# Convolution statistics from partial sums, issued one step later, and q projections pulled up beside the last LayerNorm

## The chip, the cores and the metric

The kernel runs on all eight cores of one Trainium2 chip, one batch element per core, with no exchange between cores. The metric is the device time of one launch, set by the slowest core. Such a program has a second, slower state in some executions: the cores of one die show a lower granted TensorE clock (0.834 to 0.838 in one run of the changed kernel). Ratios compare fast runs alone. A median given here is of all runs of its kernel, slow ones included, unless it is called one of fast runs. The kernel before takes 1239.6 us (median of 16 runs, 1235.1 the fastest; three of the 16 lie above 1300 us, and the median of the other 13 is 1238.8).

## The reference, cut to what matters

One encoder layer for `x` of 2048 x 1024 per core:

```python
x = layer_norm(x, ln_in_g, ln_in_b)
u = x @ w_in                                   # q | k | v | conv-GLU | gates
y_a = windowed_gqa(q, k, v, rel_bias, sink) @ w_attn_out
# conformer branch: GLU, depthwise conv of width 31, LayerNorm over 512 channels, SiLU
y_c = silu(layer_norm(depthwise(glu) + conv_b, conv_ln_g, conv_ln_b)) @ w_conv_out
mix = (sigmoid(g_a) * y_a + sigmoid(g_c) * y_c) @ w_out
# ... two more LayerNorms and a SwiGLU feed-forward ...
```

The change touches the LayerNorm of the conformer branch and the order of what follows it up to attention.

## The kernel before

A small scheduler keeps one list of operations per engine and derives semaphores from what each operation reads and writes. Every engine works through its own list in order. An operation that waits holds up everything behind it on its engine. Names: `pe` is TensorE, `act` ScalarE, `dve` VectorE, `pool` GpSimd. `tc` counts four blocks of 512 tokens, `cc` four tiles of 128 channels. A PSUM bank is one 128 x 512 fp32 piece of the memory into which TensorE writes its products; to evict it is to copy it out, after which TensorE may use it again.

```python
for tc in range(4):                            # one convolution block
    for cc in range(4):
        pb = 4 + (cc % 2)                      # two PSUM banks
        # pe: 31 matmuls with diagonal weights into bank(pb)
        # act: dv[cc] = bank(pb) + bias ; act: sqv[cc] = dv[cc]**2        [cut]
    def f_mean(e, dv=dv):                      # mean over partitions and tiles: 4 fp32 products
        for cc in range(4):
            ins = e.matmul(bank(6), onesm[:, :], dv[:, cc, :], start=(cc == 0), stop=(cc == 3))
        return ins
    sc.add("pe", f_mean, ...)                  # f_ex2: the same 4 products on sqv into bank 7
    # act: m2b = mean**2 ; dve: varb = ex2 - m2b ; act: rstdb = sqrt ; dve: reciprocal
    # per cc: dve subtract, dve multiply, act SiLU -> ycin                [cut]
# pool: memset of esf (overlays the buffers above); dve: sink terms       [cut]
for j in range(3):                             # bias tables, one staging pair
    sc.dma("sp", ... out=bstage ...)           # and mstage
    sc.add("act", ... exp(bstage) ...)
    sc.add("dve", ... expb[j] = bstage * mstage ...)
wslots = [load_w(c) for c in range(4)]         # q weights, issued by pool
for i in range(4):                             # 16 q tiles
    for tc in range(4):
        pb = nextbank(0, 4)
        proj(wslots[i], 0, 128, tc, pb, 128)   # pe: 8 matmuls
        # act: copy bank(pb) to qT                                        [cut]
# then 4 k tiles, 4 v tiles, attention; then the gates (wao, wco loads)   [cut]
```

The softmax here doesn't subtract the row's maximum and nothing guards it: scores larger than these inputs give would overflow.

Of the kernel before, what the change touches and what calls it, by code (L numbers as in the profile page):

```python
# [5 lines left out]
F32 = mybir.dt.float32  # L6
BF16 = mybir.dt.bfloat16
# [3 lines left out]
S = 2048  # L11
# [173 lines left out]
def build(debug=False):  # L185
# [80 lines left out]
    def bank(b):  # L266
        return ps[:, b * 512:(b + 1) * 512]
# [249 lines left out]
    tbuf, o = sbn(o, 2, [128, 512], F32, "tbuf")  # L517
    for tc in range(4):
# [4 lines left out]
        for cc in range(4):  # L523
            pb = 4 + (cc % 2)

            def f_conv(e, cc=cc, tc=tc, pb=pb):
                ins = None
                for j in range(31):
# [9 lines left out]
                   reads=[(dn, cc)], writes=[("sq", cc)])  # L538

        def f_mean(e, dv=dv):  # L540
            ins = None
            for cc in range(4):
                ins = e.matmul(bank(6), onesm[:, :], dv[:, cc, :], start=(cc == 0), stop=(cc == 3))
            return ins
        sc.add("pe", f_mean, reads=[(dn, c) for c in range(4)] + ["onesm"], writes=[("ps", 6)])

        def f_ex2(e, sqv=sqv):
            ins = None
            for cc in range(4):
                ins = e.matmul(bank(7), onesm[:, :], sqv[:, cc, :], start=(cc == 0), stop=(cc == 3))  # L550
            return ins
        sc.add("pe", f_ex2, reads=[("sq", c) for c in range(4)] + ["onesm"], writes=[("ps", 7)])
        sc.add("act", lambda e: e.activation(m2b[:, :], bank(6), AF.Square), reads=[("ps", 6)], writes=["m2b"])
        sc.add("dve", lambda e: e.tensor_tensor(varb[:, :], bank(7), m2b[:, :], ALU.subtract),  # L554
               reads=[("ps", 7), "m2b"], writes=["varb"])
        sc.add("act", lambda e: e.activation(rstdb[:, :], varb[:, :], AF.Sqrt, bias=epsc[:, 0:1]),
               reads=["varb", "epsc"], writes=["rstdb"])
        sc.add("dve", lambda e: e.reciprocal(rstdb[:, :], rstdb[:, :]), reads=["rstdb"], writes=["rstdb"])
        for cc in range(4):
            tb = tbuf[cc % 2]  # L560
            tn = "tbuf%d" % (cc % 2)
            sc.add("dve", lambda e, cc=cc, tb=tb, dv=dv: e.tensor_tensor(tb[:, :], dv[:, cc, :], bank(6), ALU.subtract),
                   reads=[(dn, cc), ("ps", 6)], writes=[tn])
            sc.add("dve", lambda e, tb=tb: e.tensor_tensor(tb[:, :], tb[:, :], rstdb[:, :], ALU.mult),
                   reads=[tn, "rstdb"], writes=[tn])
            sc.add("act", lambda e, cc=cc, tc=tc, tb=tb: e.activation(
                ycv[:, cc, tc * 512:(tc + 1) * 512], tb[:, :], AF.Silu,
                bias=small[:, C_CONVLB + cc:C_CONVLB + cc + 1], scale=small[:, C_CONVG + cc:C_CONVG + cc + 1]),
                reads=[tn, "small"], writes=[("ycin", cc)])
    dbg_dump("d_ycin", ycin, 128, 4 * S)  # L570

    o = MT_OFF
    qT, o = sb(o, [128, 8 * S], BF16, "qT")
    assert o <= AD_OFF
# [9 lines left out]
    NP = 9  # L584
    pTb, o = sbn(o, NP, [128, 512], BF16, "pT")
# [3 lines left out]
    qTv = qT[:, :].rearrange("p (h s) -> p h s", h=8)  # L589
# [9 lines left out]
    sc.add("act", lambda e: e.activation(esink[0:64, :], small[0:64, C_SINK:C_SINK + 8], AF.Exp),  # L599
           reads=["small"], writes=["esink"])  # L600
    sc.add("pool", lambda e: e.memset(esf[0:64, :], 0.0), writes=["esf"])
    for h in range(8):
        sc.add("dve", lambda e, h=h: e.tensor_scalar(esfv[0:64, h, :], esfv[0:64, h, :], esink[0:64, h:h + 1],
                                                      None, ALU.add), reads=["esf", "esink"], writes=["esf"])
    sc.add("dve", lambda e: e.tensor_copy(esh[0:1, :], esf[0:1, :]), reads=["esf"], writes=["esh"])
    sc.add("dve", lambda e: e.tensor_tensor(esf[0:1, :], esf[0:1, :], esh[0:1, :], ALU.subtract),
           reads=["esf", "esh"], writes=["esf"])
    sc.add("dve", lambda e: e.tensor_copy(esl[0:1, :], esf[0:1, :]), reads=["esf"], writes=["esl"])
    for j in range(3):
        sc.dma("sp", lambda e, j=j: e.dma_start(out=bstage[:, :], in_=bias_d[j]), writes=["bstage"])  # L610
        sc.dma("sp", lambda e, j=j: e.dma_start(out=mstage[:, :], in_=mask_d[j]), writes=["mstage"])
        sc.add("act", lambda e: e.activation(bstage[:, :], bstage[:, :], AF.Exp), reads=["bstage"], writes=["bstage"])
        sc.add("dve", lambda e, j=j: e.tensor_tensor(expbv[:, j, :], bstage[:, :], mstage[:, :], ALU.mult),
               reads=["bstage", "mstage"], writes=["expb"])

    pctr = [0]

    def nextbank(lo, n):
        b = lo + pctr[0] % n
        pctr[0] += 1  # L620
        return b

    wslots = [load_w(c) for c in range(4)]
    sk_ = None
    for i in range(4):
        s_ = wslots[i]
        if i == 1:
            sk_ = load_w(4)
        if i == 2:
            sv_ = load_w(5)  # L630
# [510 lines left out]
```

## Time and profile before

| what | value |
|---|---|
| time, median of 16 runs | 1239.6 us |
| profiled run | 1235.1 us, cores 1219.7 to 1233.6 |
| mean over cores, first convolution matmul to first attention matmul (QK) | 216.8 us |
| mean over cores, first QK to first product with v | 3.38 us |

The profiled run is the fastest of the sixteen. The last row is read from each core's TensorE timeline; I call it "the stretch". The lines that show how it is filled stand in the prediction.

### The profile page before, as it was taken

Reading aid. Unit: us, or ns where it says so; the run is one execution under the profiler, and the core shown is the slowest. Engines: PE = TensorE matmul, PEld = TensorE weight load, DVE = VectorE, ACT = ScalarE, POOL = GpSimd, SP = SyncE. Lnnn points to the kernel's source line nnn. Section 1 sums busy time; section 2 is a strip of 40 time slices with the busy share of each in tenths; the row PEclk is TensorE's granted clock in tenths of the full one; section 3 lists DMA queues with packets and bytes.
Section 4 is the critical chain, followed back from the end, with each engine's and each line's share of the span. In section 5 each row is a group of like instructions: output and inputs, shape, how many; then the busy total and the mean of one; then the engine's idle time right before and its main releaser. Section 6 shows DMA issues by size and latency. Waiting matters only on the chain.

```text
span 1233.6 us, 14722 instructions; the slowest of 8 cores (1219.7 to 1233.6 us)
## 1 busy us (share of the span) xinstructions
PE 1057.2 (86%) x4836; PEld 465.6 (38%) x4836; DVE 509.3 (41%) x702; ACT 411.0 (33%) x575; POOL 209.3 (17%) x318
## 2 busy tenths in 40 slices
PE   0778999965999959999963998998989899999994
PEld 0334444422523324444421443443434344444441
DVE  6663022223079812222273454254534454252224
ACT  2463133323379912222215225122341315221111
POOL 1010000001034412323210322011210212103200
PEclk9989999986979969999985999999999999999997
DMA  9762000005200051313080999357860858429901
GB/s 223 178 139 41 1 1 1 18 0 137 44 1 18 13 108 18 69 35 52 1 205 1 160 152 169 65 109 165 131 109 32 191 88 141 62 66 176 152 1 69
DMA packets 44762, 102.92 MB, mean 83 GB/s; under 512 B 5072, under 2 KB 6736, under 8 KB 44304
## 3 DMA queue, kind: packets, MB, share of 16 engines
q0 software_dynamic: 34848, 68.07, 35.1%
q1 hardware_dynamic: 9840, 33.90, 8.4%
q8 instruction: 41, 0.67, 0.2%
q14 instruction: 33, 0.27, 0.1%
HBM read 159.27 MB, written 8.39 MB: 136 GB/s over the span
## 4 chain that ended last, share of the span: by engine, by line
PE 69%; DMA 11%; DVE 8%; ACT 6%; issue 5%; POOL 0%; SPq 0%; DVEq 0%; ACTq 0%; POOLq 0%
PE ps L973 18%; PE ps L381 15%; PE ps L1007 12%; PE ps L529 5%; PE ps L880 3%; PE ps L784 2%; PE ps L775 2%; DMA xtA<-x 2%; PE ps L700 2%; PE ps L671 2%; DMA xtE<-x 2%; DMA wE<-wg 2%; PE ps L708 2%; DMA wdn<-wd 2%; DVE xtE L933 1%
## 5 line engine op out<-in xcount | busy, mean ns | idle before, releaser
L973 PE MATMUL ps<-mT,wE 128*128 128x512 bf16 x1408 | 312.3, 381 | 8.4 <-DMA wE<-wg 5.9
L381 PE MATMUL ps<-x0T,wbuf 128*128 128x512 bf16 x800 | 197.2, 403 | 39.3 <-DMA wbuf<-win 21.4
L973 PEld LDWEIGHTS ps<-mT,wE 128*128 128x128 bf16 x1408 | 137.2, 98 | 175.7 <-issue 17.0
L1007 PE MATMUL ps<-wdn,hid 128*128 128x512 bf16 x704 | 152.6, 379 | 4.4 <-DVE hid L981 3.0
L381 PEld LDWEIGHTS ps<-x0T,wbuf 128*128 128x128 bf16 x800 | 81.2, 102 | 146.7 <-issue 63.2
L981 DVE TENSOR_TENSOR hid<-ps,sgb 128x512 bf16<-128x512 f32 x88 | 60.4, 690 | 163.9 <-PE ps L973 140.7
L979 ACT ACTIVATE sgb<-ps 128x512 f32<-128x512 f32 x88 | 51.7, 593 | 186.2 <-PE ps L973 186.1
L529 PE MATMUL ps<-glu,diag 128*128 128x512 bf16 x496 | 108.4, 379 | 3.4 <-ACT dwb L534 3.4
L308 POOL DMA_DIRECT2D wE<-wg x88 | 46.6, 529 | 342.5 <-PE ps L973 338.5
L1007 PEld LDWEIGHTS ps<-wdn,hid 128*128 128x128 bf16 x704 | 68.6, 98 | 88.4 <-issue 6.3
L880 PE MATMUL ps<-wout,mT 128*128 128x512 bf16 x256 | 66.2, 419 | 19.3 <-DVE xtE L891 19.3
L686 DVE TENSOR_TENSOR pT<-E,expb 128x512 bf16<-128x512 f32 x61 | 59.8, 1017 | 40.5 <-ACT E L680 37.1
L798 DVE TENSOR_TENSOR t<-ps,gab 128x512 f32<-128x512 f32 x32 | 22.1, 692 | 130.3 <-PE ps L775 130.3
L529 PEld LDWEIGHTS ps<-glu,diag 128*128 128x128 bf16 x496 | 47.9, 97 | 64.3 <-issue 6.5
L308 POOL DMA_DIRECT2D wE<-wu x88 | 46.6, 529 | 106.7 <-PE ps L973 92.4
L802 POOL TENSOR_TENSOR mT<-t,t 128x512 bf16<-128x512 f32 x32 | 40.4, 1262 | 122.3 <-DVE t L800 122.3
L792 ACT ACTIVATE gab<-ps,small 128x512 f32<-128x512 f32 x32 | 22.0, 688 | 101.1 <-PE ps L381 101.1
L1013 DVE SCALAR_TENSOR_TENSOR zb<-xtE,ps 128x512 f32<-128x512 f32 x32 | 22.0, 686 | 80.6 <-PE ps L1007 80.6
L686 POOL TENSOR_TENSOR pT<-E,expb 128x512 bf16<-128x512 f32 x31 | 39.4, 1272 | 77.7 <-ACT E L680 76.0
L880 PEld LDWEIGHTS ps<-wout,mT 128*128 128x128 bf16 x256 | 26.8, 106 | 56.9 <-issue 33.0
L680 ACT ACTIVATE E<-ps 128x512 f32<-128x512 f32 x92 | 47.5, 580 | 0.5 <-POOL pT L686 0.5
L554 DVE TENSOR_TENSOR varb<-ps,m2b 128x512 f32<-128x512 f32 x4 | 2.8, 692 | 104.0 <-PE ps L550 104.0
(112 smaller groups left out, 1069.1 us busy)
## 6 DMA issues: line engine op xcount, KB each, us to landing
wE<-wg POOLq DMA_DIRECT2D x88, 256.0 KB, 5.6
wE<-wu POOLq DMA_DIRECT2D x88, 256.0 KB, 5.7
xtA<-x SPq DMA_DIRECT2D x16, 512.0 KB, 8.9
xtE<-x SPq DMA_DIRECT2D x16, 512.0 KB, 13.3
out<-zb SPq DMA_DIRECT2D x16, 512.0 KB, 2.8
wbuf<-win POOLq DMA_DIRECT2D x26, 256.0 KB, 5.2
wdn<-wd POOLq DMA_DIRECT2D x11, 512.0 KB, 11.5
lnp<-lnp SPq DMA_DIRECT2D x3, 1024.0 KB, 9.5
```

The costliest lines, as they stand in the source:

```text
L308: sc.dma("pool", lambda e: e.dma_start(out=dst_ap, in_=src_ap), reads=reads, writes=writes)
L381: ins = e.matmul(bank(pb)[0:prows, :], w[:, kc, c0:c1], x0Tv[:, kc, tc * 512:(tc + 1) * 512], start=(kc == 0), stop=(kc == 7))
L529: ins = e.matmul(bank(pb), diagv[:, cc, j, :], gluv[:, cc, tc * 512 + j:tc * 512 + j + 512], start=(j == 0), stop=(j == 30))
L671: sc.add("pe", lambda e, g=g, kb=kb, n=n, pb=pb: e.matmul(bank(pb).rearrange("p (a b q) -> p a b q", a=2, b=2), kTv[0:64, g, kb * 128:(kb ...
L680: sc.add("act", lambda e, Et=Et, pb=pb: e.activation(Et[:, :], bank(pb), AF.Exp, scale=0.125), reads=[("ps", pb)], writes=["E%d" % ei])
L686: sc.add(mul_eng, lambda e, Et=Et, pt=pt, j=j, g=g: e.tensor_tensor(pt[:, :], Et[:, :], expbv[:, j, g * 512:(g + 1) * 512], ALU.mult), rea ...
L802: sc.add("pool", lambda e, t1=t1, t2=t2, f=f, tc=tc: e.tensor_tensor(mTv[:, f, tc * 512:(tc + 1) * 512], t1[:, :], t2[:, :], ALU.add), rea ...
L880: ins = e.matmul(bank(pb), mTv[:, kc, t * 128:(t + 1) * 128], woutv[:, kc, half * 512:(half + 1) * 512], start=(kc == 0), stop=(kc == 7))
L973: ins = e.matmul(bank(pb), w[:, kc, :], mTv[:, kc, ST * 512:(ST + 1) * 512], start=(kc == 0), stop=(kc == 7))
L979: sc.add("act", lambda e, sg=sg, bg=bg: e.activation(sg[:, :], bank(bg), AF.Silu), reads=[("ps", bg)], writes=["sgb%d" % i2])
L981: sc.add("dve", lambda e, sg=sg, bu=bu, ffc=ffc: e.tensor_tensor(hidv[:, ffc, :], bank(bu), sg[:, :], ALU.mult), reads=[("ps", bu), "sgb%d ...
L1007: ins = e.matmul(bank(pb), hidv[:, k, tl * 128:(tl + 1) * 128], wdnv[:, k, half * 512:(half + 1) * 512], start=(k == 0), stop=(k == NFF - 1))
```

## The change

The intent is to leave no time between convolution and attention in which TensorE idles, and to take work off it. In this diff, and in those of the experiments, dots and plain words stand for code that is not shown.

```diff
+    wslots = [load_w(c) for c in range(4)]        # q weights asked for before the convolution
+    def qtile(n): ...                             # issue the next n q tiles and their copies
     for tc in range(4):
-            pb = 4 + (cc % 2)
+            pb = (4, 5, 0, 1)[cc]
 ...
+            # cc = 1, 2, 3: dve dsum += dv[cc] ; pool qsum += sqv[cc]      [cut]
+            if cc == 0 and tc > 0:
+                stat_fn[tc - 1]()                 # statistics of the block before
-        f_mean: 4 products on dv ; f_ex2: 4 products on sqv
+        def stats(tc=tc, ...):
+            if tc == 3:
+                qtile(2)
+            sc.add("pe", ... matmul(bank(6), onesm, dsum) ...)
+            sc.add("pe", ... matmul(bank(7), onesm, qsum) ...)
             # m2b, varb, sqrt, reciprocal as before
+            if tc == 3:
+                qtile(4)
             for cc in range(4):
                 # subtract, multiply, SiLU as before
+                if tc == 3:
+                    qtile(1)
+    stat_fn[3]()
 ...
-    for j in range(3): bias DMA, exp, multiply    # one staging pair, ahead of the q tiles
+    const_dma(0); const_dma(1)                    # two staging pairs
+    qtile(2); const_a(); qtile(4)                 # const_a: memset and sink terms
+    const_exp(0); const_dma(2)
     # k tiles
+    const_exp(1)
     # v tiles
+    const_exp(2)
```

More of the change, by code (lines that the diff above doesn't have):

```diff
@@ L517, in build, with nextbank, qtile @@
     tbuf, o = sbn(o, 2, [128, 512], F32, "tbuf")
+    dsum, o = sbn(o, 1, [128, 512], F32, "dsum")
+    qsum, o = sbn(o, 1, [128, 512], F32, "qsum")
+    stat_fn = {}
+    wslots = [load_w(c) for c in range(4)]
+    qT, _ = sb(MT_OFF, [128, 8 * S], BF16, "qT")
+    qTv = qT[:, :].rearrange("p (h s) -> p h s", h=8)
+    pctr = [0]
+    def nextbank(lo, n):
+        b = lo + pctr[0] % n
+        pctr[0] += 1
+        return b
+    qlist = [(i, tc) for i in range(4) for tc in range(4)]
+    wkv = {}
+    def qtile(n):
+        for _ in range(n):
+            i, tc = qlist.pop(0)
+            if tc == 0 and i in (1, 2):
+                wkv[i] = load_w(3 + i)
+            pb = nextbank(0, 4)
+            proj(wslots[i], 0, 128, tc, pb, 128)
+            sc.add("act", lambda e, i=i, tc=tc, pb=pb: e.copy(qTv[:, i, tc * 512:(tc + 1) * 512], bank(pb)),
+                   reads=[("ps", pb)], writes=[("qT", i)])
+            if tc == 3:
+                sc.dma("sp", lambda e, i=i: e.dma_start(out=qTv[0:64, 4 + i, :], in_=qTv[64:128, i, :]),
+                       reads=[("qT", i)], writes=[("qT", 4 + i)])
     for tc in range(4):
@@ L538, in build @@
                    reads=[(dn, cc)], writes=[("sq", cc)])
-        def f_mean(e, dv=dv):
-            ins = None
-            for cc in range(4):
-                ins = e.matmul(bank(6), onesm[:, :], dv[:, cc, :], start=(cc == 0), stop=(cc == 3))
-            return ins
-        sc.add("pe", f_mean, reads=[(dn, c) for c in range(4)] + ["onesm"], writes=[("ps", 6)])
-        def f_ex2(e, sqv=sqv):
-            ins = None
-            for cc in range(4):
-                ins = e.matmul(bank(7), onesm[:, :], sqv[:, cc, :], start=(cc == 0), stop=(cc == 3))
-            return ins
@@ L552, in build @@
-        sc.add("pe", f_ex2, reads=[("sq", c) for c in range(4)] + ["onesm"], writes=[("ps", 7)])
-        sc.add("act", lambda e: e.activation(m2b[:, :], bank(6), AF.Square), reads=[("ps", 6)], writes=["m2b"])
-        sc.add("dve", lambda e: e.tensor_tensor(varb[:, :], bank(7), m2b[:, :], ALU.subtract),
-               reads=[("ps", 7), "m2b"], writes=["varb"])
-        sc.add("act", lambda e: e.activation(rstdb[:, :], varb[:, :], AF.Sqrt, bias=epsc[:, 0:1]),
-               reads=["varb", "epsc"], writes=["rstdb"])
@@ L558, in build @@
-        sc.add("dve", lambda e: e.reciprocal(rstdb[:, :], rstdb[:, :]), reads=["rstdb"], writes=["rstdb"])
-        for cc in range(4):
-            tb = tbuf[cc % 2]
-            tn = "tbuf%d" % (cc % 2)
-            sc.add("dve", lambda e, cc=cc, tb=tb, dv=dv: e.tensor_tensor(tb[:, :], dv[:, cc, :], bank(6), ALU.subtract),
-                   reads=[(dn, cc), ("ps", 6)], writes=[tn])
-            sc.add("dve", lambda e, tb=tb: e.tensor_tensor(tb[:, :], tb[:, :], rstdb[:, :], ALU.mult),
-                   reads=[tn, "rstdb"], writes=[tn])
-            sc.add("act", lambda e, cc=cc, tc=tc, tb=tb: e.activation(
-                ycv[:, cc, tc * 512:(tc + 1) * 512], tb[:, :], AF.Silu,
-                bias=small[:, C_CONVLB + cc:C_CONVLB + cc + 1], scale=small[:, C_CONVG + cc:C_CONVG + cc + 1]),
-                reads=[tn, "small"], writes=[("ycin", cc)])
+            ds, qs = dsum[0], qsum[0]
@@ new lines, in build @@
+            if cc == 1:
+                sc.add("dve", lambda e, dv=dv, ds=ds: e.tensor_tensor(ds[:, :], dv[:, 0, :], dv[:, 1, :], ALU.add),
+                       reads=[(dn, 0), (dn, 1)], writes=["dsum0"])
+                sc.add("pool", lambda e, sqv=sqv, qs=qs: e.tensor_tensor(
+                    qs[:, :], sqv[:, 0, :], sqv[:, 1, :], ALU.add),
+                    reads=[("sq", 0), ("sq", 1)], writes=["qsum0"])
+            elif cc > 1:
+                sc.add("dve", lambda e, dv=dv, ds=ds, cc=cc: e.tensor_tensor(
+                    ds[:, :], ds[:, :], dv[:, cc, :], ALU.add),
+                    reads=["dsum0", (dn, cc)], writes=["dsum0"])
+                sc.add("pool", lambda e, sqv=sqv, qs=qs, cc=cc: e.tensor_tensor(
+                    qs[:, :], qs[:, :], sqv[:, cc, :], ALU.add),
+                    reads=["qsum0", ("sq", cc)], writes=["qsum0"])
@@ new lines, in build, with stats @@
+            if cc == 0 and tc > 0:
+                stat_fn[tc - 1]()
+        def stats(tc=tc, dv=dv, sqv=sqv, dn=dn):
+            if tc == 3:
+                qtile(2)
+            sc.add("pe", lambda e: e.matmul(bank(6), onesm[:, :], dsum[0][:, :], start=True, stop=True),
+                   reads=["dsum0", "onesm"], writes=[("ps", 6)])
+            sc.add("pe", lambda e: e.matmul(bank(7), onesm[:, :], qsum[0][:, :], start=True, stop=True),
+                   reads=["qsum0", "onesm"], writes=[("ps", 7)])
+            sc.add("act", lambda e: e.activation(m2b[:, :], bank(6), AF.Square), reads=[("ps", 6)], writes=["m2b"])
+            sc.add("dve", lambda e: e.tensor_tensor(varb[:, :], bank(7), m2b[:, :], ALU.subtract),
+                   reads=[("ps", 7), "m2b"], writes=["varb"])
+            sc.add("act", lambda e: e.activation(rstdb[:, :], varb[:, :], AF.Sqrt, bias=epsc[:, 0:1]),
+                   reads=["varb", "epsc"], writes=["rstdb"])
+            sc.add("dve", lambda e: e.reciprocal(rstdb[:, :], rstdb[:, :]), reads=["rstdb"], writes=["rstdb"])
+            if tc == 3:
+                qtile(4)
+            for cc in range(4):
+                tb = tbuf[cc % 2]
+                tn = "tbuf%d" % (cc % 2)
+                sc.add("dve", lambda e, cc=cc, tb=tb: e.tensor_tensor(
+                    tb[:, :], dv[:, cc, :], bank(6), ALU.subtract), reads=[(dn, cc), ("ps", 6)], writes=[tn])
+                sc.add("dve", lambda e, tb=tb: e.tensor_tensor(tb[:, :], tb[:, :], rstdb[:, :], ALU.mult),
+                       reads=[tn, "rstdb"], writes=[tn])
+                sc.add("act", lambda e, cc=cc, tb=tb: e.activation(
+                    ycv[:, cc, tc * 512:(tc + 1) * 512], tb[:, :], AF.Silu,
+                    bias=small[:, C_CONVLB + cc:C_CONVLB + cc + 1], scale=small[:, C_CONVG + cc:C_CONVG + cc + 1]),
+                    reads=[tn, "small"], writes=[("ycin", cc)])
+                if tc == 3:
+                    qtile(1)
@@ L570, in build @@
+        stat_fn[tc] = stats
+    stat_fn[3]()
     dbg_dump("d_ycin", ycin, 128, 4 * S)
-    o = MT_OFF
-    qT, o = sb(o, [128, 8 * S], BF16, "qT")
-    assert o <= AD_OFF
     o = PH_OFF
@@ L584, in build @@
     NP = 9
+    PT_OFF = o
     pTb, o = sbn(o, NP, [128, 512], BF16, "pT")
@@ L588, in build @@
     esl, o = sb(o, [128, 1024], BF16, "esl")
-    qTv = qT[:, :].rearrange("p (h s) -> p h s", h=8)
     qT4 = qT[:, :].rearrange("p (a b s) -> p a b s", a=2, b=4)
@@ L597, in build @@
     expbv = expb[:, :].rearrange("p (j c) -> p j c", j=3)
-    sc.add("act", lambda e: e.activation(esink[0:64, :], small[0:64, C_SINK:C_SINK + 8], AF.Exp),
-           reads=["small"], writes=["esink"])
-    sc.add("pool", lambda e: e.memset(esf[0:64, :], 0.0), writes=["esf"])
-    for h in range(8):
-        sc.add("dve", lambda e, h=h: e.tensor_scalar(esfv[0:64, h, :], esfv[0:64, h, :], esink[0:64, h:h + 1],
-                                                      None, ALU.add), reads=["esf", "esink"], writes=["esf"])
@@ L605, in build @@
-    sc.add("dve", lambda e: e.tensor_copy(esh[0:1, :], esf[0:1, :]), reads=["esf"], writes=["esh"])
-    sc.add("dve", lambda e: e.tensor_tensor(esf[0:1, :], esf[0:1, :], esh[0:1, :], ALU.subtract),
-           reads=["esf", "esh"], writes=["esf"])
-    sc.add("dve", lambda e: e.tensor_copy(esl[0:1, :], esf[0:1, :]), reads=["esf"], writes=["esl"])
-    for j in range(3):
-        sc.dma("sp", lambda e, j=j: e.dma_start(out=bstage[:, :], in_=bias_d[j]), writes=["bstage"])
-        sc.dma("sp", lambda e, j=j: e.dma_start(out=mstage[:, :], in_=mask_d[j]), writes=["mstage"])
-        sc.add("act", lambda e: e.activation(bstage[:, :], bstage[:, :], AF.Exp), reads=["bstage"], writes=["bstage"])
-        sc.add("dve", lambda e, j=j: e.tensor_tensor(expbv[:, j, :], bstage[:, :], mstage[:, :], ALU.mult),
-               reads=["bstage", "mstage"], writes=["expb"])
@@ L616, in build @@
-    pctr = [0]
-    def nextbank(lo, n):
-        b = lo + pctr[0] % n
-        pctr[0] += 1
-        return b
-    wslots = [load_w(c) for c in range(4)]
-    sk_ = None
-    for i in range(4):
-        s_ = wslots[i]
-        if i == 1:
-            sk_ = load_w(4)
-        if i == 2:
-            sv_ = load_w(5)
-        for tc in range(4):
-            pb = nextbank(0, 4)
-            proj(s_, 0, 128, tc, pb, 128)
-            sc.add("act", lambda e, i=i, tc=tc, pb=pb: e.copy(qTv[:, i, tc * 512:(tc + 1) * 512], bank(pb)),
-                   reads=[("ps", pb)], writes=[("qT", i)])
-        sc.dma("sp", lambda e, i=i: e.dma_start(out=qTv[0:64, 4 + i, :], in_=qTv[64:128, i, :]),
-               reads=[("qT", i)], writes=[("qT", 4 + i)])
+    bst2, _ = sb(PT_OFF, [128, 1024], F32, "bst2")
@@ new lines, in build, with const_dma, const_exp @@
+    mst2, _ = sb(PT_OFF + 4096, [128, 1024], F32, "mst2")
+    bms = [(bstage, "bstage", mstage, "mstage"), (bst2, "bst2", mst2, "mst2")]
+    def const_dma(j):
+        bs, bn, ms, mn = bms[j % 2]
+        sc.dma("sp", lambda e: e.dma_start(out=bs[:, :], in_=bias_d[j]), writes=[bn])
+        sc.dma("sp", lambda e: e.dma_start(out=ms[:, :], in_=mask_d[j]), writes=[mn])
+    def const_exp(j):
+        bs, bn, ms, mn = bms[j % 2]
+        sc.add("act", lambda e: e.activation(bs[:, :], bs[:, :], AF.Exp), reads=[bn], writes=[bn])
+        sc.add("dve", lambda e: e.tensor_tensor(expbv[:, j, :], bs[:, :], ms[:, :], ALU.mult),
+               reads=[bn, mn], writes=["expb"])
@@ new lines, in const_a @@
+    def const_a():
+        sc.add("act", lambda e: e.activation(esink[0:64, :], small[0:64, C_SINK:C_SINK + 8], AF.Exp),
+               reads=["small"], writes=["esink"])
+        sc.add("pool", lambda e: e.memset(esf[0:64, :], 0.0), writes=["esf"])
+        for h in range(8):
+            sc.add("dve", lambda e, h=h: e.tensor_scalar(esfv[0:64, h, :], esfv[0:64, h, :], esink[0:64, h:h + 1],
+                                                          None, ALU.add), reads=["esf", "esink"], writes=["esf"])
+        sc.add("dve", lambda e: e.tensor_copy(esh[0:1, :], esf[0:1, :]), reads=["esf"], writes=["esh"])
+        sc.add("dve", lambda e: e.tensor_tensor(esf[0:1, :], esf[0:1, :], esh[0:1, :], ALU.subtract),
+               reads=["esf", "esh"], writes=["esf"])
+        sc.add("dve", lambda e: e.tensor_copy(esl[0:1, :], esf[0:1, :]), reads=["esf"], writes=["esl"])
@@ L638, in build @@
+    const_dma(0)
+    const_dma(1)
+    qtile(2)
+    sk_, sv_ = wkv[1], wkv[2]
+    const_a()
+    qtile(4)
+    const_exp(0)
+    const_dma(2)
     for tc in range(4):
```

## The prediction

> **What bounds the kernel now.** I read the cores first (span and clock), then the page's engine shares, then the chain that ended last, then TensorE's waits and its timeline in the stretch that the change touches. From the page and the cores view:
>
> ```profile
> PE 1057.2 (86%) x4836; PEld 465.6 (38%) x4836; DVE 509.3 (41%) x702; ACT 411.0 (33%) x575; POOL 209.3 (17%) x318
> ...
> PE 69%; DMA 11%; DVE 8%; ACT 6%; issue 5%; POOL 0%; SPq 0%; DVEq 0%; ACTq 0%; POOLq 0%
> ...
> core 3: 1222.8 us, clock 0.950
> ...
> core 7: 1233.6 us, clock 0.942
> ```
>
> TensorE carries the kernel: 86% busy and 69% of the chain. So time is won only where TensorE idles or does work that can be dropped. The other engines have room (GpSimd 17%). The cores lie within 1.1%, so this is a fast run; I work on core 7, the slowest.
>
> The change touches one stretch: depthwise convolution with its LayerNorm statistics, then the q, k and v projections, up to the first attention matmul (QK). TensorE's timeline there, from one convolution block to attention (columns: start, duration, what, idle before it):
>
> ```profile
> 193.60 13.57 PE L529 MATMUL ps<-glu,diag 128*128 128x512 bf16 x62
> 208.32 13.57 PE L529 MATMUL ps<-glu,diag 128*128 128x512 bf16 x62 [1.14 <-ACT dwb L534]
> 222.93 3.67 PE L543 MATMUL ps<-dwb,onesm 128*128 128x512 f32 x8 [1.04 <-ACT dwb L534]
> 226.43 3.60 PE L550 MATMUL ps<-sq,onesm 128*128 128x512 f32 x8
> 229.87 13.57 PE L529 MATMUL ps<-glu,diag 128*128 128x512 bf16 x62
> ...
> 262.70 3.60 PE L550 MATMUL ps<-sq,onesm 128*128 128x512 f32 x8
> 285.17 9.95 PE L381 MATMUL ps<-x0T,wbuf 128*128 128x512 bf16 x32 [18.88 <-DMA wbuf<-win]
> 300.95 29.62 PE L381 MATMUL ps<-x0T,wbuf 128*128 128x512 bf16 x128 [5.83 <-ACT qT L634]
> 330.40 7.31 PE L654 MATMUL ps<-wbuf,x0T 128*128 128x128 bf16 x128
> 337.64 2.74 PE L671 MATMUL ps<-qT,kT 64*128 64x512 bf16 x7
> ```
>
> The reader sees three losses. A convolution block repeats every 229.87 - 193.60 = 36.27 us, though its 124 matmuls need only 26.8. Two of the missing 9.4 us are waits on ScalarE, 7 are the fp32 statistics. After the last block TensorE stands 18.88 us, then 5.83 us more. And it comes back slow: the first 32 projection matmuls take 9.95 us, where 32 at the later pace (0.216 us each) take 6.9.
>
> The two idle spells have causes in other queues:
>
> ```profile
> 278.55 0.94 POOL L601 MEMSET esf<- 64x1024 f32 x1 [172.64 <-DVE tbuf L562]
> ...
> 279.44 2.11 POOL L308 DMA_DIRECT2D wbuf<-win  x4
> ...
> 299.27 1.06 ACT L612 ACTIVATE bstage<-bstage 128x1024 f32<-128x1024 f32 x1 [5.42 <-DMA bstage<-biasT]
> 300.23 2.03 ACT L634 CAST qT<-ps 128x512 bf16<-128x512 f32 x4
> ```
>
> GpSimd issues the q weight loads behind a memset of `esf`, which waits for the last VectorE use of the memory it overlays. So the loads start at 279.4, although their buffers were free at about 122. The second spell is ScalarE: it waits in program order for the third bias table (one staging buffer, reloaded three times) and only then evicts the first four q tiles, so the four PSUM banks stay full.
>
> **What the Trainium skill says.**
> - "FP8 and Floating Point Precision", TensorE Precision Notes: true fp32 is 4 passes through the array. The trace agrees in size: eight trace records for four fp32 products take 3.5 us, 0.875 us per product against 0.216 for bf16, a ratio of 4.05.
> - "TensorE: Matmul & The Clock Gate", What's actually happening: an idle window of about 3.4 us halves TensorE's clock, and about 3.4 us of work restores it. The stretches agree: granted clock 0.73 from 258.2 to 285.2 and 0.88 in the rest of the projections, against 1.00 in the convolution. So filling the gap also removes a slow restart.
> - "GPSIMD Engine Reference", Performance versus the Vector engine: an element-wise operation with two inputs is about twice as slow there as on VectorE. The trace agrees: 1262 ns on GpSimd (mT) against some 690 on VectorE for 128x512 fp32. The three new adds per block on GpSimd should cost 1.3 us each.
>
> **The change part by part**, in us of TensorE's time from the first convolution matmul (122.5) to the first attention matmul (337.64), 215.1 now:
>
> 1. *Statistics.* The four channel tiles are summed before TensorE averages over partitions: VectorE adds the values, GpSimd the squares, three adds each per block. Per block 2 fp32 products stay of 8: 6 x 0.875 = 5.25 saved, 21.0 over four blocks. The adds (12 x 0.7 on VectorE, 12 x 1.3 on GpSimd) lie beside the convolution. VectorE is busy 28 of 136 us there, GpSimd not at all.
> 2. *Statistics later, more PSUM banks.* The statistics of a block are issued after the first channel tile of the next one (6.7 us of matmuls), and the convolution uses four banks instead of two. The last square is ready about 0.9 (eviction) + 0.7 (square) + 1.5 (GpSimd add) = 3 us after the block ends, before the 6.7 us are over, so both waits (1.04 and 1.14) should go: 4 x 1.04 + 3 x 1.14 = 7.6. ScalarE evicts the second tile of a block only after the previous LayerNorm chain, at about 22 us into the block; its bank is next written at 33, so that holds nothing up.
> 3. *q projections pulled up.* The weights are requested before the convolution. Two q tiles (3.5 us) cover the wait for the last sums, four more (6.9) the square root and reciprocal (1.28 + 0.72 + 3.35), four more the normalisation, which is paced by VectorE's 1.4 us per tile against 1.73 of matmul. Gone: 18.88 of idle.
> 4. *Bias tables.* A second staging pair, and the exponentials spread between the projections, so q evictions no longer sit behind them: 5.83 of idle gone.
> 5. *Restart.* 160 matmuls took 9.95 + 29.62 less a little overlap, 39.4; at 0.216 they need 34.5: 4.9 gone.
>
> Sum: 21.0 + 7.6 + 18.9 + 5.8 + 4.9 = 58.2. Built up from work alone the new stretch is 496 x 0.2164 = 107.3 convolution, 8 x 0.875 = 7.0 statistics, 34.5 for 20 q and k tiles and 7.3 for v: 156.1, so 59.0 less. The ways agree within 1 us.
>
> What comes back: the third table's exponential now stands after the v evictions, and the first products of attention need the whole table. ScalarE gives 1.06 and VectorE 1.2 us there, so I charge 2 us at the start of attention, and 1 us for small stalls of the q tiles. Expected: 58.5 - 3 = 55.5 us. The other cores' stretches, first convolution to first QK, run from 214.8 (core 3) to 218.8 (core 5), so the slowest core gains no less than the fastest.
>
> **The rivals.**
> - *Given back at the next weight load.* After attention all cores wait for wao and wco (5.75 and 5.90 idle on core 7), loaded only when attention ends. If the loads came at a fixed time, the gain would shrink there. But they are released by the attention buffers, so they move up with it. If the cores now arrive more nearly together and contend harder, I estimate 2 to 5 us lost, from the 4 us by which their attention starts now differ: 1185 to 1188.
> - *ScalarE becomes the bound of the tail.* It evicts q and runs the LayerNorm in the same 17 us. Its work there is about 10 x 0.6 evictions, 4 x 0.8 SiLU, two table loads of 1.28 and 2.6 of squares and root: some 14 us. Near full, and waits on VectorE's chain come on top. If q tiles stall behind it, 5 to 8 us return and the clock may sag: 1188 to 1192.
> - *GpSimd late.* If its adds took twice as long (contention with VectorE for memory), the sums would still be ready about 5 us after a block, inside the 6.7. Only at the last block (3.5 us of cover) would 1 or 2 us show.
> - *More throttling.* TensorE would run 156 us without a gap. The clock was 1.00 over 135 us of convolution on all cores I looked at, so this needs something new; a clock of 0.95 there would cost 8 us.
>
> **Range and chances.** 1238.2 - 55.5 is about 1182.5. The gains are idle time and dropped matmuls on the chain itself, and nothing downstream is tied to a clock time, so I trust the sign fully. Two of the rivals together (some 12 us) give the high end; the low end is the full 59 with calmer cores afterwards. Predicted 1182 us, range 1172 to 1196. Faster by over 2% means under 1213.4, which more than half of the sum already reaches: chance 0.97; within 2% 0.025; slower 0.005.
>
> **What would show it right or wrong.** In the changed kernel: (a) the two fp32 groups have 16 records in all instead of 64, in pairs of about 1.75 us per block; (b) convolution blocks repeat every 28.6 us with no wait on dwb; (c) no wait of TensorE on wbuf or qT over 1 us before attention, and clock about 1.00 from convolution to v; (d) first convolution to first QK is 156 to 160 us; (e) attention's first products wait for expb 1 to 3 us longer; (f) from the first QK to the end nothing moves by more than 5 us. I am wrong if (d) holds and the time does not fall by 50 (given back later), or if q tiles in the tail show waits on qT evictions (ScalarE bound).

## The result, and the profile after

The changed kernel takes 1178.9 us (median of 11 runs, one of them slow), against 1239.6. The medians of the fast runs alone are 1178.7 and 1238.8. The ratio is 0.9509, 95% interval 0.9486 to 0.9532. A ratio is the mean time of one kernel's fast runs over that of the other's of the same rounds, so it is not quite the ratio of the medians.

First the page of the changed kernel: engine shares, and the chain that ended last by engine.

```profile
PE 1025.2 (87%) x4788; PEld 455.0 (39%) x4788; DVE 520.0 (44%) x714; ACT 410.1 (35%) x575; POOL 225.6 (19%) x330
...
PE 74%; DMA 10%; DVE 6%; issue 4%; ACT 4%; POOL 1%; SPq 0%; DVEq 0%; ACTq 0%; POOLq 0%
```

TensorE lost 32 us of busy time and 48 matmul records. The records are the fp32 products, by estimate 24 x 0.875 = 21 us. Some 5 us more are the same projection matmuls at a higher clock; the rest is not traced, and the two pages are of different cores. VectorE and GpSimd gained 10.7 and 16.3 us, mostly the sums. TensorE's share of the chain rose from 69% to 74%.

TensorE's timeline over the same stretch (start, duration, what, idle before it), on core 1, now the slowest:

```profile
158.44 26.98 PE L556 MATMUL ps<-glu,diag 128*128 128x512 bf16 x124
185.26 1.02 PE L586 MATMUL ps<-dsum,onesm 128*128 128x512 f32 x2
186.12 1.02 PE L588 MATMUL ps<-qsum,onesm 128*128 128x512 f32 x2
186.98 26.98 PE L556 MATMUL ps<-glu,diag 128*128 128x512 bf16 x124
...
235.62 3.61 PE L381 MATMUL ps<-x0T,wbuf 128*128 128x512 bf16 x16
239.07 1.02 PE L586 MATMUL ps<-dsum,onesm 128*128 128x512 f32 x2
239.93 1.02 PE L588 MATMUL ps<-qsum,onesm 128*128 128x512 f32 x2
240.79 31.24 PE L381 MATMUL ps<-x0T,wbuf 128*128 128x512 bf16 x144
271.87 7.31 PE L691 MATMUL ps<-wbuf,x0T 128*128 128x128 bf16 x128
279.11 1.26 PE L709 MATMUL ps<-qT,kT 64*128 64x512 bf16 x4
281.45 1.35 PE L709 MATMUL ps<-qT,kT 64*128 64x512 bf16 x3 [1.07 <-ACT E L718]
284.45 0.59 PE L738 MATMUL ps<-pT,v 128*64 128x512 bf16 x2 [1.65 <-POOL pT L724]
```

No bracket stands before 281.45: TensorE never waits from the convolution to attention. Blocks repeat every 186.98 - 158.44 = 28.54 us. The stretch as one window (busy time of each engine, granted clock, DMA):

```profile
123.20:279.10 155.90, 155.90 (x801) 73.92 (x799) 55.17 (x66) 65.11 (x92) 17.84 (x15) 1.00 0.14 34
```

155.9 of 155.9 us busy at clock 1.00. It is 155.9 us on every one of the eight cores, where before it ran from 214.8 to 218.8. The price is at its end: the first product with v comes 5.34 us after the first QK, against 3.38 before.

One thing there is the same in both kernels and easy to overlook. In the first microseconds of attention the granted clock falls to 0.50 and stays there for 10 us or more while TensorE is busy without a break. Core 7 of the kernel before, same columns:

```profile
346.00:351.00 5.00, 5.00 (x12) 1.31 (x11) 3.37 (x5) 2.66 (x5) 1.37 (x2) 0.50 0.00 0
361.00:366.00 5.00, 5.00 (x22) 1.62 (x21) 4.71 (x7) 4.82 (x10) 2.52 (x2) 1.00 0.01 3
```

The only wait that its timeline shows between 300.95 and 346 is one of 0.63 us. Seven of the eight cores do this before the change and all eight after it. No run here shows why.

Means over the eight cores of the two profiled runs, in us:

| | before | changed | difference |
|---|---|---|---|
| first convolution to first QK | 216.8 | 155.9 | -60.9 |
| first QK to first product with v | 3.4 | 5.3 | +2.0 |
| from there to the first wco product | 110.2 | 111.0 | +0.8 |
| from there to the end | 777.7 | 778.5 | +0.8 |
| span | 1228.5 | 1171.1 | -57.4 |

The first row is the gain, and 3.6 us are given back, 2.0 of them at attention's start. The profiled launches differ by 1235.1 - 1178.3 = 56.8, the medians by 60.7; the profiled run of the kernel before was its fastest.

### The profile page after: what moved, and what is told of

The parts are those of the page before. It is cut to its first block, busy times and chain, and to the rows that moved or that the text cites. A ratio compares the mean times of both kernels' runs of the same rounds, so it can differ in the third digit from the quotient of the medians.

```text
span 1176.5 us, 14703 instructions; the slowest of 8 cores (1163.1 to 1176.5 us)
## 1 busy us (share of the span) xinstructions
PE 1025.2 (87%) x4788; PEld 455.0 (39%) x4788; DVE 520.0 (44%) x714; ACT 410.1 (35%) x575; POOL 225.6 (19%) x330
## 4 chain that ended last, share of the span: by engine, by line
PE 74%; DMA 10%; DVE 6%; issue 4%; ACT 4%; POOL 1%; SPq 0%; DVEq 0%; ACTq 0%; POOLq 0%
PE ps L1011 19%; PE ps L381 16%; PE ps L1045 13%; PE ps L556 9%; PE ps L918 3%; PE ps L822 2%; PE ps L813 2%; DMA xtA<-x 2%; PE ps L738 2%; PE ps L709 2%; DMA xtE<-x 2%; PE ps L746 2%; DMA wdn<-wd 2%; DVE xtE L971 1%; DMA wE<-wu 1%
## 5 line engine op out<-in xcount | busy, mean ns | idle before, releaser
L381 PE MATMUL ps<-x0T,wbuf 128*128 128x512 bf16 x800 | 192.1, 396 | 16.5 <-DVE glu L414 9.1
L1011 PEld LDWEIGHTS ps<-mT,wE 128*128 128x128 bf16 x1408 | 137.7, 98 | 173.3 <-issue 13.4
L1045 PEld LDWEIGHTS ps<-wdn,hid 128*128 128x128 bf16 x704 | 68.6, 98 | 88.4 <-issue 6.3
L918 PE MATMUL ps<-wout,mT 128*128 128x512 bf16 x256 | 63.5, 405 | 20.5 <-DVE xtE L929 20.5
L308 POOL DMA_DIRECT2D wE<-wu x88 | 46.6, 529 | 105.9 <-PE ps L1011 93.5
L1051 DVE SCALAR_TENSOR_TENSOR zb<-xtE,ps 128x512 f32<-128x512 f32 x32 | 21.9, 686 | 80.3 <-PE ps L1045 80.3
L354 PE MATMUL ps<-ident,x0b 128*128 128x128 bf16 x128 | 10.9, 241 | 34.8 <-DVE x0b L470 31.1
```

The costliest lines, as they stand in the source:

```text
L308: sc.dma("pool", lambda e: e.dma_start(out=dst_ap, in_=src_ap), reads=reads, writes=writes)
L381: ins = e.matmul(bank(pb)[0:prows, :], w[:, kc, c0:c1], x0Tv[:, kc, tc * 512:(tc + 1) * 512], start=(kc == 0), stop=(kc == 7))
L918: ins = e.matmul(bank(pb), mTv[:, kc, t * 128:(t + 1) * 128], woutv[:, kc, half * 512:(half + 1) * 512], start=(kc == 0), stop=(kc == 7))
L1011: ins = e.matmul(bank(pb), w[:, kc, :], mTv[:, kc, ST * 512:(ST + 1) * 512], start=(kc == 0), stop=(kc == 7))
L1045: ins = e.matmul(bank(pb), hidv[:, k, tl * 128:(tl + 1) * 128], wdnv[:, k, half * 512:(half + 1) * 512], start=(k == 0), stop=(k == NFF - 1))
```

## The experiments

Theory: the stretch is bound by TensorE's list alone, each part removes a different holder of it (something that keeps TensorE waiting), and nothing downstream takes the gain back. Rivals: one part does it all; the parts are the same wait counted several times; or the gain is partly returned at the next weight loads. Four runs undo one part each in the changed kernel, one splits a part, two add parts to the kernel before, and the rest test what the parts cost and what comes after them. "The stretch" is the mean of the eight cores in the run's profile, but for one run where this is said. "Over the changed kernel" is the difference of the medians.

**Undo the partial sums.** Eight products per block again, on `dv` and `sqv`; a second buffer for the squares keeps the later order legal.

```diff
-            sc.add("pe", ... matmul(bank(6), onesm, dsum) ...)
+            sc.add("pe", f_mean, ...)      # 4 products on dv; f_ex2: 4 on sqv; no dsum, qsum
```

> The changed kernel with only the partial sums undone: TensorE again averages all four tiles (8 fp32 products per block instead of 2; the squares get a second buffer so that the later order stays legal). If the products lie on TensorE's path, 24 of them at 0.875 us return: +21 us over the changed kernel, 1200 us, ratio to before 0.968. If instead they would hide in other engines' work (VectorE and GpSimd carry less now), under +8 us: below 1187.

Measured 1199.8 us, ratio 0.9689 (0.9661 to 0.9718): 20.9 over the changed kernel. The stretch is 176.5, 20.6 longer. One block of its timeline:

```profile
152.00 3.60 PE L578 MATMUL ps<-dwb,onesm 128*128 128x512 f32 x8
155.43 3.60 PE L585 MATMUL ps<-sq,onesm 128*128 128x512 f32 x8
```

The products sit on TensorE's path one for one: the two groups hold the convolution up for 6.87 us (152.00 to 158.87, where it resumes) instead of 1.71.

**Undo the later issue and the two extra banks.**

```diff
-            pb = (4, 5, 0, 1)[cc]
+            pb = 4 + (cc % 2)
-            if cc == 0 and tc > 0:
-                stat_fn[tc - 1]()
-        stat_fn[tc] = stats
-    stat_fn[3]()
+        stats()
```

> The changed kernel with only the later issue undone: statistics straight after their block, two PSUM banks for the convolution; the partial sums stay. My theory: TensorE now waits for the last square's GpSimd add, about 3 us per block, and at the third channel tile for ScalarE, about 1.5 us; three blocks show it, the last is covered by q tiles: +13 us, 1192. That would mean that the sums alone give back most of what they save. Rival, the order hardly matters because the waits in the kernel before were only 1.1 us each: at most +6 us, 1185.

Measured 1194.0 us (one of four runs slow, left out of the ratio 0.9644, 0.9606 to 0.9682). The stretch is 167.6, 11.7 longer. TensorE's timeline around one block:

```profile
182.10 1.10 PE L584 MATMUL ps<-dsum,onesm 128*128 128x512 f32 x2 [1.73 <-DVE dsum L574]
183.48 1.10 PE L586 MATMUL ps<-qsum,onesm 128*128 128x512 f32 x2 [0.29 <-POOL qsum L577]
184.42 13.57 PE L556 MATMUL ps<-glu,diag 128*128 128x512 bf16 x62
199.13 13.57 PE L556 MATMUL ps<-glu,diag 128*128 128x512 bf16 x62 [1.14 <-ACT dwb L561]
```

The sums alone make a wait of 1.73 + 0.29 us where the kernel before waited 1.04, and the wait of 1.14 on the third tile stays. So the rival that order hardly matters falls. A block repeats every 184.42 - 152.10 = 32.3 us (the block before resumed at 152.10): the sums alone bring 36.3 down to 32.3, the order and the two banks take it to 28.5. No run parts the order from the banks.

**Undo the early q weights and tiles.**

```diff
-    wslots = [load_w(c) for c in range(4)]        # before the convolution
-                qtile(2) ... qtile(4) ... qtile(1)    # inside stats
-    qtile(2)
     const_a()
-    qtile(4)
+    wslots = [load_w(c) for c in range(4)]
+    qtile(16)
```

> The changed kernel with the q weights and q tiles back at their old place (weights issued after the memset that waits for VectorE, all 16 tiles after the LayerNorm chain of the last block); sums, order and bias staging stay. Theory: an idle gap of about 19 us before the first q tile, 3 us wait for the last sums, and 3 to 5 us of slow clock: +23 us, 1202. Rival, the bias tables were the real holder of the gap and are spread out now: under +12 us.

Measured 1209.6 us, ratio 0.9771 (0.9737 to 0.9805), 30.6 over the changed kernel where I expected 23; the stretch is 183.2, 27.3 longer. From its TensorE timeline:

```profile
234.22 1.10 PE L583 MATMUL ps<-dsum,onesm 128*128 128x512 f32 x2 [1.84 <-DVE dsum L573]
235.49 1.10 PE L585 MATMUL ps<-qsum,onesm 128*128 128x512 f32 x2 [0.18 <-POOL qsum L576]
258.11 37.35 PE L381 MATMUL ps<-x0T,wbuf 128*128 128x512 bf16 x160 [21.52 <-DMA wbuf<-win]
```

The idle is 21.5 us on this core and not 19, and the 160 projection matmuls take 37.35 us instead of 34.5, at a granted clock of 0.93 instead of 1.00. It is the part that costs most to undo. The direction was right, the size 4 us too small in the stretch.

**Undo only half of it: weights early, tiles late.**

```diff
-                qtile(2) ... qtile(4) ... qtile(1)    # inside stats
-    qtile(2)
+    qtile(12)
```

> The changed kernel with the weights requested early as it does, but all q tiles after the LayerNorm chain of the last block in every engine's order. It parts the two halves of step 3. Theory: TensorE waits 3 us for the last sums, fills four banks with q tiles, and waits some 6 us until ScalarE is through the chain: +9 us, 1188. Rival A, only the weights' lateness mattered: within 2 us of the changed kernel. Rival B, only the order mattered: about as slow as with both undone, 1200.

The time is inconclusive: two of the four runs were slow and the two others 1192.2 and 1208.5. The profile itself fell in the slow state: cores 4 and 5, of die 1, show clocks of 0.922 and 0.934 and stretches of 173.5 and 173.3. So I read only die 0, whose cores have stretches of 169.0, 168.9, 167.8 and 168.0: 12.5 longer than 155.9 (expected 9). On core 0 TensorE waits 1.84 us for the sums, does four tiles, then stands 7.59 us until ScalarE evicts one. So the place of the tiles costs 12.5 us, and late weights on top of it the other 14.8 of the 27.3: about half each, undone in this order. (The run before this one also put the sink terms ahead of the tiles; what that does alone was not tested.) Neither rival holds.

**Undo the spread bias tables.**

```diff
-    const_dma(0); const_dma(1); qtile(2); const_a(); qtile(4); const_exp(0); const_dma(2)
+    const_a()
+    for j in range(3):
+        const_dma(j); const_exp(j)                # one staging pair
+    qtile(6)
```

> The changed kernel with only the bias tables as before: one staging pair, three exponentials in a row on ScalarE ahead of the last six q evictions. Theory: ScalarE stands for three table loads one after another (about 6 us each from the end of the LayerNorm chain), TensorE fills its four banks and waits 8 to 10 us, plus 2 us of slow clock, less the 2 us that the late third table costs the changed kernel at the start of attention: +9 us, 1188. Rival, with q tiles pulled up the tables hide by themselves: within 2 us of the changed kernel.

Measured 1193.8 us, ratio 0.9638 (0.9609 to 0.9667): 14.9 over the changed kernel. The stretch is 17.3 longer, and 2.0 come back after it (first QK to v again 3.38). I had expected 9. ScalarE's timeline shows why:

```profile
259.06 1.06 ACT L650 ACTIVATE bstage<-bstage 128x1024 f32<-128x1024 f32 x1 [2.63 <-DMA bstage<-biasT]
267.75 1.06 ACT L650 ACTIVATE bstage<-bstage 128x1024 f32<-128x1024 f32 x1 [7.64 <-DMA bstage<-biasT]
274.67 1.06 ACT L650 ACTIVATE bstage<-bstage 128x1024 f32<-128x1024 f32 x1 [5.86 <-DMA bstage<-biasT]
275.63 2.03 ACT L540 CAST qT<-ps 128x512 bf16<-128x512 f32 x4
```

The first exponential starts at 259.06, and the other two follow 8.7 and 6.9 us later; I had expected about 6 each, counted from the end of the LayerNorm chain (the last SiLU ends at 254.24). The first multiply on VectorE, which frees the staging pair, starts at 262.33, behind the sink terms. TensorE stands 15.2 us. So with everything else changed the tables do not hide by themselves. The run undoes the second staging pair and the spreading together, and moves the sink terms two tiles forward.

**One line alone.** The kernel before with the weights requested early.

```diff
+    wslots = [load_w(c) for c in range(4)]        # before the convolution
     for tc in range(4):
```

> The kernel before, with one line moved: the q weights are requested before the convolution. The 18.9 us wait on them goes. Theory: ScalarE, which must go through the chain and three bias tables before it evicts a q tile, becomes the holder: TensorE does four tiles and waits until about 300 us again, so nearly nothing is won, 0 to -3 us, 1237. Rival, a wait of 18.9 us taken from the chain shows in full: 1220.

Measured 1238.0 us, ratio 0.9973 (0.9925 to 1.0022). The stretch falls by 1.6 us. TensorE's timeline:

```profile
261.99 3.60 PE L551 MATMUL ps<-sq,onesm 128*128 128x512 f32 x8
265.42 7.07 PE L381 MATMUL ps<-x0T,wbuf 128*128 128x512 bf16 x32
300.26 29.92 PE L381 MATMUL ps<-x0T,wbuf 128*128 128x512 bf16 x128 [27.77 <-ACT qT L634]
```

The wait of 18.88 us on the weights is gone, and 27.77 us on the q eviction have taken its place. TensorE resumes at 300 as it did before.

**Two together.** The same with the spread bias tables in addition.

```diff
-    for j in range(3): bias DMA, exp, multiply
+    const_dma(0); const_dma(1)                    # exps after the q, k and v tiles
```

> The kernel before with the early q weights of the run before this one and, in addition, the spread bias tables; statistics and order of q tiles stay as before. Early weights alone won 1.6 us of the stretch from first convolution to first QK. If weights and tables are two holders of one gap, taking both away must win far more than the sum of each alone: TensorE then waits only for the LayerNorm chain on ScalarE, about 7 us after four tiles, so 18 us less, 1220. If the chain itself is the holder, about -3 us, 1236.

Measured 1222.5 us (one of four runs slow), ratio 0.9851 (0.9830 to 0.9872), 17 us less than before. The stretch is 194.9, 21.9 shorter; 3.3 us are lost between first QK and v, where TensorE waits 3.56 us for the copy of kT. The two holders stand behind the same tiles: the early weights alone win 1.6, both together 21.9. The spread tables alone were not run on the kernel before. TensorE now stands 7.58 us for ScalarE, a wait that is gone in the changed kernel, where the tiles are interleaved, and back (7.59) in the run above where they are late.

**Squares on VectorE instead of GpSimd.**

```diff
-                sc.add("pool", ... qs + sqv[cc] ...)
+                sc.add("dve", ... qs + sqv[cc] ...)
```

> The changed kernel with the sums of squares on VectorE instead of GpSimd. The sums lie beside 6.7 us of convolution, or 3.5 us of q tiles at the last block, and are ready after about 3 us either way: same as the changed kernel within 2 us. Rival, GpSimd's adds slow the path (or relieve VectorE's chain): over 4 us of difference.

Measured 1180.2 us (one of five runs slow) against 1178.5 of the changed kernel on the same chip; ratios to the kernel before 0.9511 (0.9495 to 0.9526) and 0.9507. The stretch is 155.9 again. Which engine adds the squares is of no account here.

**Third table earlier.**

```diff
+        if tq == 1:                               # after the second v eviction
+            const_exp(2)
-    const_exp(2)
```

> The changed kernel with the third table's exponential after the second v eviction instead of the fourth. Theory: the 2 us that attention's start lost (first QK to first product with v 3.38 us before, 5.34 us in the changed kernel) come back: 1177. Rival, the start of attention is bound by the slow clock there or by other engines: no change.

First QK to first product with v falls from 5.34 to 3.55 us in the profile, 1.8 of the expected 2. Two of six runs were slow. The median of the four fast ones is 1174.3, 4.4 less than the changed kernel's 1178.7, but the interval of the ratio (0.9415 to 0.9527) does not resolve so little. The trace also has 107.8 us instead of 111.0 from there to the first wco product. Four of the eight cores keep a clock of 1.00 from 284 to 294, where all cores of the changed kernel fell to 0.50 early in attention. So the late table may cost more than its 2 us; one profile doesn't show that.

**Gate weights requested during attention.** A test of the argument that the next loads move up with attention because only buffers hold them back.

```diff
+    wao, _ = sb(PH_OFF + 24576, ...)              # where the bias staging lay
+    wcoA, _ = sb(PH_OFF + 32768, ...)             # where esf lay; wcoB loaded after attention
     for i, (n, g) in enumerate(units):
         ...
+        if i == 12:
+            prefetch_gate()                       # 2 win chunks, 2 halves of wao, half of wco
```

> The changed kernel with the gate stage's weights (two win chunks, wao, half of wco) requested in the middle of attention, into room that the bias staging has left. It tests whether the waits after attention are tied to attention's end by buffers (as I argued against the first rival). Theory: 2.4 + 6.7 + 6.6 us of idle and some 4 us of slow clock go, and a few us return because GpSimd issues the loads between attention's products: -14 us, 1165. Rival, the loads slow attention, or memory bandwidth gives the time back at the next load: within 4 us of the changed kernel.

Measured 1172.9 us, ratio 0.9454 (0.9408 to 0.9501), 6 us won instead of 14. The interval overlaps that of the changed kernel, but the trace agrees: 103.9 us instead of 111.0 from the first product with v to the first wco product. GpSimd's timeline in the middle of attention, and ScalarE's, show where the rest is:

```profile
326.45 0.55 POOL L308 DMA_DIRECT2D wao<-wao  x1
334.85 0.53 POOL L308 DMA_DIRECT2D wao<-wao  x1 [7.84 <-DMA wao<-wao]
```

```profile
337.29 1.57 ACT L718 ACTIVATE E<-ps 128x512 f32<-128x512 f32 x3 [8.43 <-POOL pT L724]
```

Both halves of wao carry one name in the dependency tracking. So the second load waits until the first has landed, and GpSimd, which also makes a third of attention's products, stands in front of it. TensorE stood 7.56 us with it on this core. From its first product with v to the end of its last, attention takes 97.8 us on average, against 88.4 in the changed kernel.

**Both, with a name for each half.**

```diff
-            cast_load(wao[...], wao_d[...], ["wao"])
+            cast_load(wao[...], wao_d[...], [("wao", i)])
```

> The early third table together with the gate weights requested during attention, this time with a separate mark for each half of wao: in the run before, GpSimd stood 7.84 us in the middle of attention because the second half waited for the first to land, and attention stood with it. If that stall ate the missing half of the gain, the gate stage's waits now show in full: 14 us for the loads and 2 for the table, 1163. If memory or attention gives the time back anyway, it stays near 1171.

Measured 1158.5 us (one of five runs slow), ratio 0.9344 (0.9330 to 0.9359): 20 us under the changed kernel, where I expected 16. The changed kernel ran on the same chip:

> The changed kernel again, on the same chip as the three others, so that a few us can be compared: 0.951 of the kernel before, some 1179 us.

That one measured 1178.5, ratio 0.9507 (0.9493 to 0.9522). In the faster kernel the time from the first product with v to the first wco product is 93.5 us against 110.8, and the first products of the gate stage follow attention without a bracket:

```profile
372.16 5.31 PE L381 MATMUL ps<-x0T,wbuf 128*128 128x512 bf16 x16
377.31 1.03 PE L822 MATMUL ps<-oT,wao 128*128 128x512 bf16 x4
378.18 0.59 PE L831 MATMUL ps<-ycin,wcoA 128*128 128x512 bf16 x2
378.61 0.59 PE L831 MATMUL ps<-ycin,wcoB 128*128 128x512 bf16 x2
```

Attention itself is back at 87.7 us. So the missing part of the gain was the stall that the first version made, and memory did not take it back. From the first wco product to the end the profile has 773.3 us instead of 779.6; nothing here explains those 6 us. All kernels gave the reference's result.

## Why the prediction was right

It said 1182 us in a range of 1172 to 1196; measured 1178.9.

- *Statistics, 21.0.* Undoing the sums costs 20.6 in the stretch. 16 fp32 records stand in the trace, in pairs of 1.71 us per block. GpSimd's adds took 1.26 to 1.47 us (1.3 was expected).
- *Later issue and banks, 7.6.* Blocks repeat at 28.54 us (28.6 was expected) with no wait. The part is worth more than my 7.6 once the sums are there (11.7), because the sums themselves would bring a longer wait than the one they replace. The 7.6 counted only the waits of the kernel before.
- *q projections, 18.9, and restart, 4.9.* Confirmed together: undone, 27.3, the slow clock (0.93) as part of it. In the changed kernel GpSimd issues the four loads between 111.8 and 122.2; the prediction had read the buffers as free at about 122.
- *Bias tables, 5.8.* Undone they cost 15.3 net. As with the order, 5.8 was what the kernel before showed of this wait while another wait hid most of it. The four undoings add up to 76.9 in the stretch, more than the 60.9 won. Parts that hold the same tiles cannot be priced by undoing each. The prediction did not do that. It counted the waits and the dropped work of one timeline, which do not overlap (58.2), and TensorE's work alone (156.1, so 59.0 less); core 7 won 59.3, and the work met 155.9.
- *What comes back, 3.* The 2 us at attention's start are there (1.96) and explained by the third table. The 1 us for stalls of q tiles was not needed.
- *The other cores.* Core 7's stretch, on which I worked, was 215.1; the mean was 216.8, so the mean gain is 1.7 larger than core 7's.
- *Rivals.* Almost nothing returned at the gate loads (+0.8 us to the first wco product), although the cores' stretches are now equal. The prediction misread one figure here: 4 us is the spread of the stretches, not of the attention starts, which lay 6.9 us apart (counted from each core's first instruction) and still lie 5.5 us apart. So the test of contention is weaker than it looks. ScalarE did not bind: no wait on a q eviction. GpSimd's adds do not matter. In the stretch the clock stayed 1.00 on all cores.

The profiled launches differ by 56.8, so the 55.5 predicted was 1.3 off there. The medians differ by 60.7. The other 4 us lie mostly in how far the slowest core falls behind, and not in a stage that the profile missed. In 22 further fast launches of the kernel before, run beside the experiments, the mean of the eight cores' spans is 1229.3 us, only 0.8 more than in the profiled one; but the slowest core lies 9.0 us above that mean, against 5.1 in the profiled launch. For the changed kernel (11 fast launches) the two figures are 1170.5 and 6.6. So the mean core gained 58.8 us, and the slowest some 2.3 more because the cores end closer together. The prediction had no term for that, and why they do is not shown.

## What to carry to other kernels

When several engines work through ordered lists, ask of every idle spell not only what ended it but what would have ended it next: a load moved up by one line won 1.6 us where 18.9 us of waiting had been on it, and 21.9 with the next holder gone as well. Price a rearrangement from the work of the bounding engine in the stretch, or from the waits and the dropped work of one timeline, but not from what undoing each part costs: here the undoings add up to 76.9 us for 60.9 won. And give a dependency tracker a name for each piece of a buffer that is loaded separately: one shared name stopped an engine for 7.84 us.

## What the Trainium skill lacked or had wrong

- "ScalarE: Activation LUTs", What ACT_TABLE_LOAD costs: it gives some 1283 ns for the load plus a drain of some 1380 ns, 2.66 us per switch. The load is 1.28 us here. The drain does not show: in the changed kernel ScalarE's eviction ends at 258.90, the load begins at 258.92, ends at 260.20, and the next activation begins at 260.21. A switch cost 1.3 us.
- "TensorE: Matmul & The Clock Gate", Seeing it yourself: it says that a die falls to 0.81 of the clock within 5 to 20 us once three of its cores run dense matmuls on data that are not all zeros or all ones. Here each of the eight cores ran the stretch's 155.9 us without a gap at a granted clock of 1.00 in the profiled fast run. Some 107 us of that are the convolution's diagonal weights, which are mostly zeros; but in the gate stage, with full weights and random data, TensorE was busy for 114.4 to 115.0 of the 115 us from 425 to 540 on every core, again at 1.00. In one of the changed kernel's eleven further runs one die's cores averaged 0.834 to 0.838 over the whole launch (1299 us), so a lower clock occurs, but as a state of some executions.
- No page that I found accounts for the low clock at the start of attention: 0.50 from 346 to 351 on core 7 of the kernel before, with TensorE busy for all of the 5.00 us and its longest wait since 300.95 only 0.63 us.
